# A decoder trunk in split float32: one more gate/up pair and branch pair by seven products, five raw weight buffers, 59 small slots

## The chip, the cores and the metric

The kernel runs on one core of a Trainium2 chip. The metric is the device time in microseconds (us) of one execution; of several executions the median is given. TensorE is called PE, VectorE DVE, ScalarE ACT, GpSimd POOL and SyncE SP, as in the profile.

## The reference, cut to what matters

Input is one sequence of 512 tokens of width 1024, in float32. There are two layers, and each has three sub-layers with an RMS norm before and after each:

```
x += 1/2 * post(SwiGLU_1(pre(x)))                 # FFN, D_FF = 2816
h  = pre(x);  P = h @ W_in                        # HGRN2 q/f/i/gate, attention q/k/v, branch gates gA, gB
A  = HGRN2 gated linear recurrence -> W_bA        # 4 heads, 128x128 state, chunks of 64
B  = sliding-window (128) attention -> W_bB       # 8 heads, 2 KV heads, ALiBi, sinks
x += post((sigmoid(gA)*A + sigmoid(gB)*B) @ W_out)
x += 1/2 * post(SwiGLU_2(pre(x)))                 # FFN

swiglu(h) = (silu(h @ w_gate) * (h @ w_up)) @ w_down
```

D_FF = 2816 gives 22 blocks of 128 (`FT`), and the width of 1024 gives 8 (`KT`).

## The kernel before, in words

**Numbers.** Every float32 product is made of three matmuls: both operands are split into a rounded high part and the rest, and high x high, low x high and high x low are summed (`mm3`; all go through L115). An operand is split by `split()`: ACT casts it to the high part (L400), DVE subtracts to get the low part (L401). Weights come in units of 128 x 1024, are loaded by SP into raw buffers (tag `w32`, `W32` = 4 of them, 512 KB each), and are split by the weight stream `Stream`: ACT casts (L324) into a `whi` tile, and the low part `wlo` is made by DVE (L331), or by ACT and an accumulating DMA of POOL (L328, L329). There are `WS` = 6 pairs of `whi` and `wlo`. Activations and all other small tensors live in slots of 128 x 512 float32 (`big()`, tag "s", 256 KB each, `SLOTS` = 61).

**An FFN.** `ffn()` first runs `quad()`: two gate/up pairs of output blocks at once, in plain form. A plain pair is two `project()` calls of 8 x 3 matmuls of 512 columns, 48 in all, followed by `gated()`. The first FFN goes on plainly to pair `FIRST` = 7, as its norm is not known yet; the three others to pair `PLAIN` = 4. All further pairs go by `sevenths()`, called from `fast()`: a 2x2 product of halves with seven products instead of eight, on sums of weights (items a, b, c, d of the stream; DVE makes the sums, L311 to L318) and on sums of the operand halves (`pre.sums()`, four times, once for each two blocks of the operand). A pair by sevenths is 7 x 4 x 3 = 84 matmuls of 256 columns. Its p1 is copied out of PSUM by ACT (L864); DVE adds the products (L874 to L882), ACT applies SiLU (L894), and DVE multiplies (L895).

**The down projection.** `down()` multiplies the 22 gated blocks by the down weights. `both(j, 0)` takes operand blocks 2j and 2j+1 against one weight unit, 24 matmuls of 512 columns. The first four of them are plain; then `quarters()` does eight blocks by seven products (items p1 to p7, split by `quarter()`, L281 for the high and L286 for the low halves; p1 needs two items); then come the remaining `both`. With the first of these units, 16 tiles of raw weights for the quarter products are loaded into small slots (the side loads, L252). The last sevenths splits the first `EARLY` = 4 operand blocks by `early()` (L892's argument), so that the first `both` has its operands:

```
            m = sevenths(pre, early)
```

**The mixer.** Its 8 output blocks have two branch gates each. For the attention branch the first `LATE` = 8 gates are plain (`branch`), and in pairs by `branches()` from there on; for the recurrent branch all go in pairs. Each pair by `branches()` uses `sevenths()`; the operand sums are made with the last four plain ones.

**The order.** The program is written in Python order, with coroutines (`order`) for what runs beside the matmuls. A scheduler then gives every instruction its place on its engine's queue, by priorities and by when slots of each tag come free; `pin()` raises the priority of a few. The engines run these queues in order, so a changed number of slots can change the order on ACT and DVE.

**The start.** Eight tiles of the input and the first weight units are loaded in turn, then the constants: `ident`, `half_ident` (two DMAs), `dist`, `mask`, `lb_in`, `hgh`, `sink`. The first FFN's squares (L430, L431), their sums by PE and the root (L443) give the norm, which enters at L904.

Of the kernel before, what the change touches and what calls it, by code (L numbers as in the profile page):

```python
# [15 lines left out]
P = 128  # L16
# [10 lines left out]
EPS = 1e-6  # L27
LEVELS = (1, 2, 4, 8, 16, 32, 64)
MASKS = [(m, n) for b in LEVELS[:-1:2] for m, n in ((b, b), (2 * b, 2 * b), (2 * b, b))] + [(64, 64)]
SLOTS = 61  # L30

WAIT = dict(
    first=0.0, spread=2300.0, squares=1700.0, lay=34500.0, laid=770.0, normed=7600.0, final=2600.0,
    head=2600.0, level=1720.0, chunks=1270.0, blocks=350.0, norm=2370.0, gate=8000.0,
    values=1200.0, scores=2000.0, exp=9000.0, shares=4500.0, turn=1900.0, turned=3000.0, rest=1200.0, lent=3500.0, apart=4000.0, block=2000.0, pair=4000.0, att0=1260.0, att1=12300.0,
)
W32, WS, AHEAD, TAIL, PLAIN, FIRST, EARLY, LATE = 4, 6, 3, 4, 4, 7, 4, 8
TURN = 0
LEAD = 8
ORDER = ("p1", "p6", "p2", "p7", "p5", "p4", "p3")  # L40
# [5 lines left out]
def trunk(ctx: ExitStack, tc: tile.TileContext, xin, wall, gains, lbT, hgain, sinks, c_dist, c_mask, c_ident, out):  # L46
    nc = tc.nc
# [11 lines left out]
    def nm(s):  # L59
        seq[0] += 1  # L60
        return f"{s}_{seq[0]}"

    def big(dt=F32, shape=None):
        return sb.tile(shape or [P, S], dt, tag="s", name=nm("s"), bufs=SLOTS)

# [9 lines left out]
    def const(shape, name, dt=F32):  # L75
        return cp.tile(shape, dt, tag=name, name=name)
# [738 lines left out]
    def quad(pre, halves):  # L815

        o = [acc() for _ in range(4)]
        blocks = {}
        ws.pinned = halves
        for half in (0, 1) if halves else (None,):  # L820
            c = WHOLE if half is None else HALF[half]
            for k in range(KT):
                order.until(lambda: pre.have[half or 0] > k)
                for j in range(4):
                    if (k, j) not in blocks:
                        blocks[k, j] = ws.next(uses=2 if halves else 1)
                    wmm(o[j][:, c], blocks[k, j], cut(pre.h[k], c), k == 0, k == KT - 1)
            ws.pinned = False
        return o

    def project(pre):
        o = acc()
        for k in range(KT):
            wmm(o, ws.next(), pre.h[k], k == 0, k == KT - 1)
        return o
# [49 lines left out]
    def fast(pre, a, start):  # L885
        def early():
            if j == FT - 1:
                for i in range(EARLY):
                    a[i] = split(a[i])

        for j in range(start, FT):
            m = sevenths(pre, early)  # L892
            z = big(F32, [P, 2, H2])
            nc.scalar.activation(out=m[:, 0:2, :], in_=m[:, 0:2, :], func=AF.Silu)  # L894
            nc.vector.scalar_tensor_tensor(z, m[:, 0:2, :], -1.0, m[:, 2:4, :], op0=ALU.mult, op1=ALU.mult)  # L895
            a.append(z.rearrange("p i t -> p (i t)"))

    def ffn(l, n, pre, nxt, halves=True):
        a = []

        def gated(og, ou):
            z, u = big(), big()
            if first:
                pin(nc.vector.tensor_tensor(z, og, pre.rb, op=ALU.mult))  # L904
                nc.scalar.activation(out=z, in_=z, func=AF.Silu)
                nc.vector.tensor_tensor(u, ou, pre.rb, op=ALU.mult)
                nc.vector.tensor_tensor(u, u, z, op=ALU.mult)
            else:
                nc.scalar.activation(out=z, in_=og, func=AF.Silu)
                pin(nc.vector.tensor_tensor(u, ou, z, op=ALU.mult))  # L910
            a.append(u)

        first = isinstance(pre, First)
        o = quad(pre, halves)
        if first:
            o.append(project(pre))
            order.until(lambda: pre.rb is not None)
        if not first:
            pre.sums()
            pre.sums()  # L920
        for j in range(2):
            gated(o[2 * j], o[2 * j + 1])
        if first:
            gated(o[4], project(pre))
            for j in range(3, FIRST):
                if j > 3:
                    order.until(lambda: pre.laid)
                    pre.sums()
                if j == 4:
                    pre.sums()  # L930
                gated(project(pre), project(pre))
            fast(pre, a, FIRST)
        else:
            for j in range(2, PLAIN):
                pre.sums()
                gated(project(pre), project(pre))
            fast(pre, a, PLAIN)
        return down(a, FT, l, n + 1, nxt, True)
# [349 lines left out]
    pre = First()  # L1288
# [4 lines left out]
            ws.load(k + 1)  # L1293
    ident = const([P, P], "ident")
    nc.sync.dma_start(ident, c_ident)
    half_ident = const([P, 64], "half_ident")
    nc.sync.dma_start(half_ident[:64], c_ident[:64, :64])
    nc.sync.dma_start(half_ident[64:], c_ident[64:, 64:])
    dist = const([P, 256], "dist")
    nc.sync.dma_start(dist, c_dist)  # L1300
    mask = const([P, len(MASKS) - 1, 32], "mask", I32)
# [5 lines left out]
    nc.sync.dma_start(hgh, hgain.partition_broadcast(P))  # L1307
    sink = const([P, DEPTH, NH], "sink")
    nc.sync.dma_start(sink, sinks.partition_broadcast(P))
    for k in range(KT):  # L1310
        pre.add(k)
        if k in (0, 2, 4):
            ws.split()
        if k > 2:
            pre.square(k - 3)
# [42 lines left out]
    for l in range(DEPTH):  # L1358
        pre = ffn(l, 0, pre, (l, 2), halves=l > 0)
        pre = mixer(l, pre, (l, 4))  # L1360
        pre = ffn(l, 4, pre, (l + 1, 0) if l + 1 < DEPTH else None)
# [81 lines left out]
```

## Time and profile before

| | us |
|---|---|
| median of 3 runs | 2112.13 (2110.0 to 2112.33) |
| profiled execution | 2114.98 |
| its span from first to last instruction | 2113.2 |
| PE busy | 2101.1 (99%) |
| DVE busy | 1551.0 (73%) |
| ACT busy | 1124.9 (53%) |
| mean granted clock of PE | 0.998 |

Times in rows count from the start of the span. In a timeline a row has the start, the length, engine, line, operation, output and input with sizes, the count, and in brackets the idle time of the engine before it with what ended that. Matmuls overlap, so a matmul's length is more than its distance to the next. A row of the chain of waits has the start, the length and the number of instructions in a row. The stages of layer 0, as the trace shows them: first FFN to about 345 us, mixer to about 700, second FFN to about 1045; layer 1 follows likewise.

### The profile page before, as it was taken

The numbers are of one execution on the slowest core, as the hardware profiler recorded it, in microseconds if no ns is written. First come the engines' busy times: TensorE is split into PE (matmuls) and PEld (weight loads), VectorE is DVE, ScalarE is ACT, GpSimd is POOL, SyncE is SP. The second block draws the span as 40 slices with busy tenths as digits, with TensorE's granted clock in tenths as the row PEclk, the third lists the DMA queues.
The fourth block names the chain that finished last, engine by engine and source line by source line (L and its number), as shares of the span: only waits on it lengthen the run. The fifth ranks groups of instructions, "written<-read, shape, count | busy, mean of one in ns | idle before, by whom it ended". The sixth has DMA issues, their size and how long they took to land.

```text
span 2113.2 us, 35244 instructions
## 1 busy us (share of the span) xinstructions
PE 2101.1 (99%) x13549; PEld 1875.3 (89%) x13549; DVE 1551.0 (73%) x2705; ACT 1124.9 (53%) x1900; POOL 154.6 (7%) x188
## 2 busy tenths in 40 slices
PE   9999999999999999999999999999999999999998
PEld 7899988887888999998899998888778989999987
DVE  5777886767676777779587778767686767777884
ACT  6555554446445555556355556454554545555562
POOL 0111000000000011110001110000000000111000
PEclk9999999999999999999999999999999999999999
DMA  7577754321237357774437775632122553677651
GB/s 234 150 181 181 188 146 137 106 70 61 70 100 209 120 125 175 180 194 125 160 109 175 181 185 150 189 116 95 51 71 70 135 185 110 154 182 181 183 165 45
DMA packets 148072, 298.36 MB, mean 141 GB/s; under 512 B 16992, under 2 KB 74816, under 8 KB 147904
## 3 DMA queue, kind: packets, MB, share of 16 engines
q1 hardware_dynamic: 122416, 228.16, 32.8%
q0 software_dynamic: 25344, 67.91, 18.5%
q8 instruction: 106, 1.74, 0.3%
q14 instruction: 62, 0.51, 0.1%
q10 hardware_dynamic: 144, 0.05, 0.0%
HBM read 213.43 MB, written 14.73 MB: 108 GB/s over the span
## 4 chain that ended last, share of the span: by engine, by line
PE 81%; DVE 9%; ACT 5%; issue 2%; DMA 2%; SPq 1%; ACTq 0%; DVEq 0%
PE acc L115 60%; PE aux L115 19%; ACT whi L324 2%; DMA w<-wall 2%; PE aux L125 1%; DVE s L401 1%; DVE wlo L331 1%; DVE wlo L286 1%; PE acc L125 1%; ACT s L400 1%; ACT m L894 1%; ACT wlo L328 1%; SPq L241 1%; DVE tt L268 0%; DVE w L267 0%
## 5 line engine op out<-in xcount | busy, mean ns | idle before, releaser
L115 PE MATMUL acc<-s,whi 128*128 128x256 f32 (+1 forms) x4968 | 1069.9, 312 | 1.7 <-ACT whi L324 0.9
L115 PEld LDWEIGHTS acc<-s,whi 128*128 128x128 f32 x4968 | 809.9, 191 | 54.5 <-issue 2.1
L115 PE MATMUL acc<-s,wlo 128*128 128x256 f32 (+1 forms) x2484 | 770.5, 310 | 0.1
L115 PEld LDWEIGHTS acc<-s,wlo 128*128 128x128 f32 x2484 | 474.5, 191 | 25.9 <-DVE wlo L331 0.4
L324 ACT CAST whi<-w 128x1024 fp32r<-128x1024 f32 (+1 forms) x341 | 317.4, 949 | 252.2 <-PE aux L115 103.4
L115 PE MATMUL acc<-whi,s 128*128 128x512 f32 x1264 | 413.6, 393 | 0.0
L324 ACT CAST whi<-tt 128x1024 fp32r<-128x1024 f32 x154 | 161.7, 1050 | 341.4 <-DVE tt L318 188.9
L331 DVE TENSOR_TENSOR wlo<-w,whi 128x1024 fp32r<-128x1024 f32 (+1 forms) x181 | 218.5, 1216 | 134.8 <-ACT whi L324 128.4
L115 PEld LDWEIGHTS acc<-whi,s 128*128 128x128 f32 x1264 | 237.0, 188 | 55.7 <-issue 3.2
L331 DVE TENSOR_TENSOR wlo<-tt,whi 128x1024 fp32r<-128x1024 f32 x154 | 188.2, 1222 | 102.5 <-ACT whi L324 102.5
L115 PE MATMUL acc<-wlo,s 128*128 128x512 f32 x632 | 246.8, 391 | 1.0 <-DVE wlo L286 1.0
L329 POOL DMA_DIRECT2D wlo<-w x160 | 138.2, 865 | 1266.3 <-ACT wlo L328 856.7
L115 PE MATMUL aux<-s,whi 128*128 128x256 f32 x1232 | 225.1, 283 | 0.0
L115 PE MATMUL aux<-whi,s 128*128 128x512 f32 x592 | 196.8, 390 | 0.0
L115 PEld LDWEIGHTS aux<-s,whi 128*128 128x128 f32 x1232 | 192.2, 192 | 0.0
L115 PE MATMUL aux<-s,wlo 128*128 128x256 f32 x616 | 174.4, 283 | 0.1
L115 PEld LDWEIGHTS acc<-wlo,s 128*128 128x128 f32 x632 | 118.7, 188 | 25.8 <-DVE wlo L286 2.4
L115 PEld LDWEIGHTS aux<-whi,s 128*128 128x128 f32 x592 | 111.1, 188 | 22.9
L328 ACT ACTIVATE wlo<-w 128x1024 fp32r<-128x1024 f32 (+1 forms) x160 | 129.9, 845 | 0.0
L400 ACT CAST s<-s 128x512 fp32r<-128x512 f32 (+1 forms) x164 | 88.6, 581 | 65.9 <-DVE s L459 60.6
L115 PEld LDWEIGHTS aux<-s,wlo 128*128 128x128 f32 x616 | 118.3, 192 | 0.3 <-DMA wlo<-w 0.3
L115 PE MATMUL aux<-wlo,s 128*128 128x512 f32 x296 | 115.2, 389 | 0.0
(185 smaller groups left out, 2136.6 us busy)
## 6 DMA issues: line engine op xcount, KB each, us to landing
w<-wall SPq DMA_DIRECT2D x267, 512.0 KB, 3.7
wlo<-w POOLq DMA_DIRECT2D x83, 512.0 KB, 5.5
w<-wall SPq DMA_DIRECT2D x288, 128.0 KB, 3.1
wlo<-w POOLq DMA_DIRECT2D x77, 256.0 KB, 3.3
x_d<-s SPq DMA_DIRECT2D x48, 256.0 KB, 2.1
s<-x_d SPq DMA_DIRECT2D x48, 256.0 KB, 5.5
w<-wall SPq DMA_DIRECT2D x34, 256.0 KB, 2.9
s<-wall SPq DMA_DIRECT2D x64, 128.0 KB, 3.5
```

Of the source, the lines that this page charges most:

```text
L115: nc.tensor.matmul(o, lhsT, rhs, start=start, stop=stop)
L125: nc.tensor.transpose(o, src, ident)
L241: nc.sync.dma_start(w.rearrange("p (m c) -> p m c", m=4) if c is None else w[:, c], a)
L286: nc.vector.tensor_tensor(it.lo[:, h[c]], w[c], it.hi[:, h[c]].bitcast(F32), op=ALU.subtract)
L324: i = nc.scalar.copy(it.hi[:, c], w[:, c])
L328: nc.scalar.mul(it.lo[:, c], w[:, c], -1.0)
L329: nc.gpsimd.dma_start(it.lo[:, c].bitcast(F32), w[:, c], accum_op=ALU.add)
L331: nc.vector.tensor_tensor(it.lo[:, c], w[:, c], it.hi[:, c].bitcast(F32), op=ALU.subtract)
L400: nc.scalar.copy(hi, src)
L401: nc.vector.tensor_tensor(lo, src, hi.bitcast(F32), op=ALU.subtract)
L894: nc.scalar.activation(out=m[:, 0:2, :], in_=m[:, 0:2, :], func=AF.Silu)
```

## The change

`PLAIN` goes from 4 to 3: the three FFNs other than the first have one plain pair less and one more by sevenths. The operand sums that went with the two plain pairs go with the one that is left. `LATE` goes from 8 to 6: each mixer has two plain attention gates less and one more pair by `branches()`. `W32` goes from 4 to 5, that is one more raw weight buffer of 512 KB, and `SLOTS` from 61 to 59, two slots of 256 KB less. With `W32` = 5 the loop at the start also issues one more weight unit among the input tiles. The two DMAs of `half_ident` are issued after all other constants.

```diff
-SLOTS = 61
+SLOTS = 59
...
-W32, WS, AHEAD, TAIL, PLAIN, FIRST, EARLY, LATE = 4, 6, 3, 4, 4, 7, 4, 8
+W32, WS, AHEAD, TAIL, PLAIN, FIRST, EARLY, LATE = 5, 6, 3, 4, 3, 7, 4, 6
...
             for j in range(2, PLAIN):
-                pre.sums()
+                while len(pre.x56) < min(4, 2 * j):
+                    pre.sums()
                 gated(project(pre), project(pre))
             fast(pre, a, PLAIN)
...
     ident = const([P, P], "ident")
     nc.sync.dma_start(ident, c_ident)
-    half_ident = const([P, 64], "half_ident")
-    nc.sync.dma_start(half_ident[:64], c_ident[:64, :64])
-    nc.sync.dma_start(half_ident[64:], c_ident[64:, 64:])
     dist = const([P, 256], "dist")
...
     nc.sync.dma_start(sink, sinks.partition_broadcast(P))
+    half_ident = const([P, 64], "half_ident")
+    nc.sync.dma_start(half_ident[:64], c_ident[:64, :64])
+    nc.sync.dma_start(half_ident[64:], c_ident[64:, 64:])
```

Lines of the kernel after are one higher than before from L932 on.

## The prediction

> **What bounds the kernel now.** I read the page's busy shares first, then TensorE's waits, then the chain of waits, and only then the timelines of the stages that the change touches.
>
> ```profile
> span 2113.2 us, 35244 instructions
> ...
> PE 2101.1 (99%) x13549; PEld 1875.3 (89%) x13549; DVE 1551.0 (73%) x2705; ACT 1124.9 (53%) x1900; POOL 154.6 (7%) x188
> ```
>
> ```profile
> engine line waited for: us in total, times, longest us
> PE acc L125 <- DVE s L730: 2.9, 1, 2.9
> PE aux L115 <- DVE s L431: 1.1, 1, 1.1
> ...
> PE acc L115 <- DVE wlo L286: 1.0, 4, 0.3
> ...
> PE acc L115 <- DVE s L904: 0.7, 1, 0.7
> ```
>
> PE is busy for 2101.1 of 2113.2 us, so time goes only by fewer or shorter matmuls, by removing the 12 us of stalls, or by making new stalls. The last is where the risk lies, as VectorE (DVE) and ScalarE (ACT) have idle time but feed PE just in time at a few places. The profiled execution took 2114.98 us, 2.85 above the median of 2112.13; I add the sum of differences to either, and state the result against the median.
>
> **Fewer matmul columns.** The order of PE's instructions in the two built kernels differs in five places only: 48 matmuls of 512 columns become 84 of 256 in the three FFNs that start from plain pairs, and in both mixers. The chain of waits prices both forms (start, length, matmuls):
>
> ```profile
> 772.07 7.20 PE acc L115 x60
> 779.27 2.88 PE aux L115 x24
> ...
> 987.92 5.44 PE aux L115 x24
> ```
>
> A pair by sevenths is 60 + 24 matmuls in 7.20 + 2.88 = 10.08 us (0.120 each). 24 matmuls of 512 columns take 5.44 us (0.2267 each), so a plain pair is 48 x 0.2267 = 10.88. Each swap saves 0.80 and five save **4.0 us**. This is certain as long as the feeding engines keep up. The Trainium skill ("TensorE: Matmul & The Clock Gate", "Back-to-back issue gap") gives N/2.4 + 2.5 ns for an isolated gap: 215.8 and 109.2 ns, from which I estimate 5.9 us for the five; the trace shows 226.7 and 120, and the rows decide.
>
> Can DVE feed the additional sevenths? In the FFNs and in the mixer:
>
> ```profile
> 900.00:910.00 10.00, 10.00 (x85) 10.00 (x85) 7.56 (x12) 5.83 (x8) 1.73 (x2) 1.00 0.77 182
> ```
>
> ```profile
> 743.40:761.99 18.59, 18.59 (x85) 15.39 (x84) 13.71 (x24) 8.44 (x12) 0.86 (x1) 1.00 0.12 34
> ```
>
> ```profile
> 743.44 1.28 DVE L563 TENSOR_TENSOR s<-s,s 128x512 f32<-128x512 f32 x2
> ...
> 747.76 0.69 DVE L311 TENSOR_TENSOR tt<-w,w 128x512 f32<-128x512 f32 x1
> ...
> 756.22 0.68 DVE L317 TENSOR_TENSOR tt<-tt,w 128x512 f32<-128x512 f32 x1
> ...
> 758.79 1.23 DVE L331 TENSOR_TENSOR wlo<-tt,whi 128x1024 fp32r<-128x1024 f32 x1 [1.17 <-ACT whi L324]
> ```
>
> ```profile
> 555.26 0.69 DVE L1091 TENSOR_REDUCE ss<-s 128x4 f32<-128x512 f32 x1 [3.72 <-ACT s L1089]
> ...
> 568.91 0.69 DVE L1091 TENSOR_REDUCE ss<-s 128x4 f32<-128x512 f32 x1 [5.04 <-ACT s L1089]
> ```
>
> The first two are windows (columns: length, then busy PE, PEld, DVE, ACT, POOL; granted clock; DMA share; GB/s), the others DVE's timeline. In steady sevenths DVE is busy 7.56 of 10 us, so it keeps up. The first sevenths of this FFN begins at 761.99 (the window's end), and one plain pair sooner, at 751.1, after the change. The operand sums of one pair take 743.44 to 747.76, 4.3 us; two in a row end at 752.1. The third weight item's own sums and split take 3.8 more (756.22 to 760.0), until 755.9; its product is the fifth of seven, and begins 4 x 10.08 / 7 = 5.76 us after the start, at 756.9. It fits with 1 us to spare. In the mixer the earlier sums fall into idle stretches of 3.72 and 5.04 us. I cost both at nothing; without that 1 us of cover, a stall of up to 1 us in each of three FFNs.
>
> **The start.** Startup ACT and PE rows (timeline: start, length, and in brackets the idle time before and its releaser):
>
> ```profile
> 22.73 1.05 ACT L324 CAST whi<-w 128x1024 fp32r<-128x1024 f32 x1 [4.35 <-DMA w<-wall]
> 24.01 1.06 ACT L324 CAST whi<-w 128x1024 fp32r<-128x1024 f32 x1 [0.23 <-DMA w<-wall]
> ```
>
> ```profile
> 32.99 1.05 PE L115 MATMUL aux<-ones,s 128*128 128x1 f32 x8 [1.09 <-DVE s L431]
> ```
>
> ```profile
> core 0: us, PE busy (x) PEld busy (x) DVE busy (x) ACT busy (x) POOL busy (x), PEclk, DMA share, GB/s
> ...
> 31.28:34.70 3.42, 2.33 (x15) 1.77 (x14) 1.62 (x3) 3.40 (x4) 1.41 (x2) 1.00 0.90 241
> 34.70:38.11 3.41, 3.41 (x10) 2.65 (x9) 0.87 (x2) 0.85 (x2) 0.46 (x1) 0.50 1.05 239
> 38.11:41.50 3.39, 2.68 (x10) 1.59 (x9) 1.29 (x2) 2.10 (x3) 0.00 (x0) 1.00 0.90 205
> ```
>
> The fifth weight unit arrives at 22.73, the sixth at 24.01; ACT's square and DVE's L431 queue behind them, and PE waits 1.09 us at 32.99. With five raw buffers the fifth unit is loaded with the first ones, so the sixth should land when the fifth does now: 24.01 - 22.73 = 1.3 us earlier. That covers the 1.09. A second price hangs on it: after the window with that stall (PE busy 2.33 of 3.42) the granted clock is 0.50 for one window of 3.41 us, which loses 3.41 / 2, about 1.6 us as the matmuls there are counted (10 instead of some 15). After a window busy 2.68 of 3.39 the clock stays 1.00. Gain: 1.1 + 1.6, less a longer wait for L904 (0.7 now), since PE arrives sooner: between 0 and 3.4, taken as **2.3 us**. The identity halves are loaded after the small constants and first used in the mixer, hundreds of us later: nothing.
>
> **The entry of the down projection, four times.** This is where the sum turns. With 59 small slots, and side loads that ask for slots one weight unit earlier, the built order on ACT and DVE changes at the end of the last sevenths, in all four FFNs alike. Before, ACT does: copy of p1 (L864), cast of a[0] (L400), unit 2 (L324), a[1], a[2], unit 3, a[3], and then the four half casts of the first two quarter items (L281). After: units 2 and 3, the four L281, and only then L864 and the four L400. On DVE the four L286 and L874 likewise stand ahead of the four L401. ACT and DVE run in order, so the down projection's operands now queue behind the L281. The second quarter item's cast waits for a `whi` buffer whose last reader is the last product of the last sevenths, and PE's next instruction needs a[0]. The rows of before, second FFN:
>
> ```profile
> 936.97 0.35 ACT L864 COPY s<-acc 128x256 f32<-128x256 f32 x1
> 937.22 0.62 ACT L400 CAST s<-s 128x512 fp32r<-128x512 f32 x1
> ...
> 941.79 1.05 ACT L324 CAST whi<-w 128x1024 fp32r<-128x1024 f32 x1 [1.96 <-DMA w<-wall]
> 942.75 0.62 ACT L400 CAST s<-s 128x512 fp32r<-128x512 f32 x1
> 943.27 0.62 ACT L281 CAST whi<-w 128x512 fp32r<-128x512 f32 x1
> 944.16 1.34 ACT L281 CAST whi<-w 128x512 fp32r<-128x512 f32 x2 [0.28 <-DMA w<-wall]
> 946.73 0.62 ACT L281 CAST whi<-w 128x512 fp32r<-128x512 f32 x1 [1.22 <-DMA w<-wall]
> ```
>
> ```profile
> 938.83 0.69 DVE L401 TENSOR_TENSOR s<-s,s 128x512 fp32r<-128x512 f32 x1
> ...
> 944.62 0.68 DVE L874 TENSOR_TENSOR m<-acc,s 128x512 f32<-128x512 f32 x1
> 945.22 1.89 DVE L286 TENSOR_TENSOR wlo<-w,whi 128x512 fp32r<-128x512 f32 x3
> ```
>
> ```profile
> 943.15 0.28 PE L115 MATMUL aux<-s,wlo 128*128 128x256 f32 x1
> 943.27 0.40 PE L115 MATMUL acc<-whi,s 128*128 128x512 f32 x1
> ...
> 943.74 0.62 PE L115 MATMUL acc<-whi,s 128*128 128x512 f32 x2
> ```
>
> Now a[0] is ready at 937.8 (high part) and 939.5 (low part), and PE passes into the down projection at 943.27 without a gap. After, in the same coordinates: the last product ends at 943.4, and the second item's two casts start at 943.45 and 944.2 to 944.5. The later one waits for its transfer, which a fifth buffer brings a unit earlier, to where the item before it has its wait now (944.16), a little later for a side load put ahead. It takes 0.62; L864 takes 0.25 of ACT and L400 0.62, so a[0]'s high part is there at 945.6 to 945.9. DVE does the last L286 at 944.8 to 945.1, L874 0.6 later, and L401 of a[0] another 0.6 later: low part at 946.7 to 947.0. PE's third matmul, at 943.74 now, needs it: a shift of 3.0 to 3.3, taken as **3.2 us**, some 2.4 of it in one piece. From below 2.2, if DVE does not bind; from above 5.5, if the transfer comes no earlier than now (946.73). Four times 3.2 is **12.8 us**. Given back: PE's four waits for L286 (1.0 in all, about 1.6 with the weight loads), since DVE has more lead then: **-1.6**.
>
> The stall also touches the clock. One idle stretch of 1.09 us cost a half-clock window above. So did the last wait:
>
> ```profile
> 2104.00:2107.00 3.00, 0.20 (x1) 0.00 (x0) 2.30 (x5) 1.02 (x3) 0.00 (x0) 0.93 0.57 175
> ```
>
> Here the clock falls within 3 us of idle. At 2.4 us in one piece and 0.7 more, each stall should be followed by a half-clock window (1.6 us); how the stall falls on the windows can spare one. I take three of four: **+4.8**, between 0 and 9.6 (two windows each). The Trainium skill ("TensorE: Matmul & The Clock Gate", "Why this matters for your kernels") says to have no idle gaps over about 3 us, by which gaps of 2.4 us would cost nothing more; the row at 31.28 speaks against it here.
>
> **Sum.** -4.0 - 2.3 + 12.8 - 1.6 + 4.8 = **+9.7 us**: 2124.7 for the profiled execution, 2121.8 against the median.
>
> **Rivals.**
> 1. The entry stalls come, but the clock stays (a window still counts as busy with 2.4 us idle): +9.7 - 4.8 = +4.9, 2117.0. For it: after 0.7 us idle the clock stayed. Against: the two rows above. By the skill's 3 us it would be this one. Chance 0.20.
> 2. Faster: the entry is covered. This needs a[0]'s cast ahead of 943.27, that is the second item's casts before about 942, by a buffer or a transfer that I have put too late. Then -4.0 - 2.3 with the L286 waits as now: -6.3, 2105.8. It decides from an entry stall below 1.6 us (four of them eat the 6.3). Against it: the buffer that the cast waits for is read until 943.27. Chance 0.14.
> 3. Slower still: the quarter item's transfer lands as late as now, 5.5 us each, with one clock window each: -4.0 - 2.3 + 22.0 - 1.6 + 6.4 = +20.5, 2132.6. Against: the built order on SyncE issues it a unit earlier. Chance 0.08.
> 4. The stalls are at their lower bound, 2.2, without the clock, and the start gains 3.4: -4.0 - 3.4 + 8.8 - 1.6 = -0.2, 2111.9. Chance 0.08.
>
> **How the numbers follow.** Forecast 0.50, rivals 0.20, 0.14, 0.08 and 0.08. A measurement of this kernel can tell about 0.2%, or 4.2 us, from no change. Faster than that: rival 2 (0.14) and a little of 4: 0.15. Same: most of rival 4 and half of rival 1: 0.17. Slower: the rest, 0.68. The range goes from 2108 (above rival 2, most of which it leaves out, below rival 4) to 2128 (3.5 us a stall, a clock window for all four and a second for one, the start gaining nothing: -4.0 + 14.0 - 1.6 + 8.0 = +16.4), leaving out rival 3. The likeliest case's own range is 2117 to 2128.
>
> **What would show it.** Right: PE's waits list four new ones of 2 to 3 us at the first matmul of the down projections, for ACT L400, and shorter ones for DVE L401; the L286 waits are gone; the clock is 0.5 in a window behind each entry; a sevenths pair still takes 10.08 us, and the wait for L431 at 33 us is gone. Wrong: ACT's L400 of a[0] ends before PE's last product of the last sevenths, or PE's busy time falls by other than 4 us apart from the clock.

## The result: 3.2% slower, and the profile after

The changed kernel took 2178.51 us in the median (2175.37 to 2182.08), against 2112.23 for before in the same executions. The ratio is 1.0316 (95% interval 1.0293 to 1.0339), slower by 66 us. The forecast was 2121.8, with a range of 2108 to 2128. One execution of the run e7 below (3737.6 us) and one of before beside e12 and e13 (2559.2) ran at a mean granted clock of 0.75 to 0.76, and all medians here leave them out. The profiled execution took 2175.55 us. Its page, and PE's waits (total, times, longest):

```profile
span 2173.8 us, 35753 instructions
...
PE 2113.3 (97%) x13729; PEld 1890.6 (87%) x13729; DVE 1574.3 (72%) x2745; ACT 1136.0 (52%) x1925; POOL 162.9 (7%) x198
```

```profile
PE acc L115 <- DMA wlo<-w: 27.3, 18, 4.8
PE acc L115 <- ACT s L400: 10.4, 4, 4.2
PE aux L115 <- ACT s L1049: 6.4, 4, 2.2
PE acc L125 <- DVE s L730: 2.8, 1, 2.8
PE aux L115 <- DMA wlo<-w: 2.8, 4, 1.1
PE acc L115 <- DVE s L401: 1.2, 3, 0.5
...
PE acc L115 <- DVE s L904: 0.7, 1, 0.7
```

Three groups of waits are new. The four waits for L400 and three for L401, at the entries of the down projections, were forecast. The other two are not in the prediction at all: 30 us for the low parts of weights, which come by POOL's accumulating DMA (L329), and 6.4 us in the mixers for L1049, a copy that attention's matmuls need. The waits for L431 and L286 are gone.

The forecast entry looks as described. ACT, then DVE, then PE in the second FFN:

```profile
963.13 1.14 ACT L281 CAST whi<-w 128x512 fp32r<-128x512 f32 x2 [1.82 <-PE aux L115]
964.52 1.14 ACT L281 CAST whi<-w 128x512 fp32r<-128x512 f32 x2 [0.25 <-PE aux L115]
965.57 0.36 ACT L864 COPY s<-acc 128x256 f32<-128x256 f32 x1
965.83 2.18 ACT L400 CAST s<-s 128x512 fp32r<-128x512 f32 x4
```

```profile
963.78 2.69 DVE L286 TENSOR_TENSOR wlo<-w,whi 128x512 fp32r<-128x512 f32 x4 [1.22 <-ACT whi L281]
966.38 0.69 DVE L874 TENSOR_TENSOR m<-acc,s 128x512 f32<-128x512 f32 x1
966.99 2.49 DVE L401 TENSOR_TENSOR s<-s,s 128x512 fp32r<-128x512 f32 x4
```

```profile
964.33 0.28 PE L115 MATMUL aux<-s,wlo 128*128 128x256 f32 x1
966.50 0.50 PE L115 MATMUL acc<-whi,s 128*128 128x512 f32 x1 [1.90 <-ACT s L400]
966.84 0.57 PE L115 MATMUL acc<-wlo,s 128*128 128x512 f32 x1
967.72 0.80 PE L115 MATMUL acc<-whi,s 128*128 128x512 f32 x1 [0.31 <-DVE s L401]
```

PE's first matmul of the down projection comes 2.2 us after the last of the sevenths, and its third at 967.72 instead of some 964.9 (964.33 and the 0.59 us that lie between the two in before): 2.8 us late, where 3.2 was forecast. The windows at the first FFN's entry show the clock's part (columns as in the prediction):

```profile
243.27:246.68 3.41, 1.64 (x6) 1.07 (x7) 3.07 (x6) 2.88 (x6) 0.00 (x0) 1.00 0.86 263
246.68:250.09 3.41, 3.41 (x10) 2.64 (x9) 2.62 (x6) 0.81 (x2) 0.00 (x0) 0.50 0.88 267
```

A window with PE busy for 1.64 of 3.41 us is followed by one at half clock. Ahead of its last matmuls, after has nine such windows, and before has one (at 34.70). Five follow the four entries, two the longer wait of each mixer (557.29 and 1639.31), and two the waits for low parts at 813.75 and 847.98.

PE's idle time grew from 12.1 to 60.5 us of the span, by 48.4, and its busy time by 12.2, in which the windows at half clock are counted. Where the 60.6 us between the two spans arise shows when each matmul of after is set beside the same one of before, as their order is the same but for the five swaps. The table gives how much later PE comes out of each part than it went in:

| part | forecast, us | after, us |
|---|---|---|
| start | -2.3 | -2.8 |
| entries of the four down projections, with the clock | +17.6 | +20.9 |
| rest of the down projections (the L286 waits) | -1.6 | -2.9 |
| mixers, with their two swaps | -1.6 | +9.1 |
| gate/up pairs of the last three FFNs, with their three swaps | -2.4 | +34.6 |
| last wait and what follows PE's last matmul | 0 | +1.7 |

### The profile page after: what moved, and what is told of

Its sections match the earlier page's. It is cut to its first block, busy times and chain, and to the rows that moved or that the text cites. A ratio compares the mean times of both kernels' runs of the same rounds, so it can differ in the third digit from the quotient of the medians.

```text
span 2173.8 us, 35753 instructions
## 1 busy us (share of the span) xinstructions
PE 2113.3 (97%) x13729; PEld 1890.6 (87%) x13729; DVE 1574.3 (72%) x2745; ACT 1136.0 (52%) x1925; POOL 162.9 (7%) x198
## 5 line engine op out<-in xcount | busy, mean ns | idle before, releaser
L115 PE MATMUL acc<-whi,s 128*128 128x512 f32 x1264 | 418.4, 398 | 11.6 <-ACT s L400 10.4
L324 ACT CAST whi<-tt 128x1024 fp32r<-128x1024 f32 x164 | 171.7, 1047 | 387.9 <-DVE tt L318 261.6
L331 DVE TENSOR_TENSOR wlo<-w,whi 128x1024 fp32r<-128x1024 f32 (+1 forms) x171 | 207.1, 1217 | 134.6 <-ACT whi L324 130.2
L331 DVE TENSOR_TENSOR wlo<-tt,whi 128x1024 fp32r<-128x1024 f32 x164 | 200.6, 1223 | 92.0 <-ACT whi L324 87.8
L329 POOL DMA_DIRECT2D wlo<-w x170 | 146.4, 863 | 1296.4 <-ACT wlo L328 857.1
L115 PE MATMUL aux<-s,whi 128*128 128x256 f32 x1312 | 239.8, 283 | 0.0
L115 PEld LDWEIGHTS aux<-s,whi 128*128 128x128 f32 x1312 | 204.6, 192 | 0.0
L115 PE MATMUL aux<-s,wlo 128*128 128x256 f32 x656 | 186.0, 284 | 2.8 <-DMA wlo<-w 2.8
L328 ACT ACTIVATE wlo<-w 128x1024 fp32r<-128x1024 f32 (+1 forms) x170 | 142.8, 847 | 0.0
L400 ACT CAST s<-s 128x512 fp32r<-128x512 f32 (+1 forms) x164 | 87.6, 579 | 85.0 <-DVE s L459 82.4
L115 PEld LDWEIGHTS aux<-s,wlo 128*128 128x128 f32 x656 | 125.9, 192 | 3.6 <-DMA wlo<-w 3.6
```

What stands on the lines that cost most here:

```text
L115: nc.tensor.matmul(o, lhsT, rhs, start=start, stop=stop)
L324: i = nc.scalar.copy(it.hi[:, c], w[:, c])
L328: nc.scalar.mul(it.lo[:, c], w[:, c], -1.0)
L329: nc.gpsimd.dma_start(it.lo[:, c].bitcast(F32), w[:, c], accum_op=ALU.add)
L331: nc.vector.tensor_tensor(it.lo[:, c], w[:, c], it.hi[:, c].bitcast(F32), op=ALU.subtract)
L400: nc.scalar.copy(hi, src)
```

## The experiments

All times are medians, and those of before, taken beside them, are 2111.4 to 2112.9. Differences to before, in us:

| kernel | time | difference | ratio, 95% interval |
|---|---|---|---|
| after | 2178.5 | +66 | 1.0293 to 1.0339 |
| e1: PLAIN = 3 alone | 2138.9 | +27.5 | 1.0114 to 1.0144 |
| e2: five raw buffers and 59 slots alone | 2124.3 | +13.0 | 1.0047 to 1.0077 |
| e3: LATE = 6 alone | 2121.3 | +9.9 | 1.0032 to 1.0062 |
| e4: after, SiLU behind the cast of a | 2181.4 | +70 | 1.0310 to 1.0344 |
| e5: e1, L874 behind L318 | 2119.2 | +6.3 | 1.0016 to 1.0039 |
| e6: after, L874 behind L318 | 2139.2 | +26.4 | 1.0115 to 1.0145 |
| e7: after, three orders | 2121.1 | +8.3 | 1.0024 to 1.0053 |
| e8: as e7, four buffers, 61 slots | 2126.5 | +13.6 | 1.0048 to 1.0078 |
| e9: five buffers, 59 slots, late identity halves and entry order, PLAIN = 4, LATE = 8 | 2108.4 | -4.5 | 0.9967 to 0.9985 |
| e10: e5 with three sums first | 2118.5 | +5.6 | 1.0015 to 1.0036 |
| e11: e9 with PLAIN = 3 as in e10 | 2113.1 | +0.2 | 0.9990 to 1.0008 |
| e12: after with LATE = 8 | 2154.4 | +41.9 | 1.0184 to 1.0221 |
| e13: after with four buffers, 59 slots | 2158.5 | +46.0 | 1.0200 to 1.0233 |

**e1, e2, e3: each constant by itself.** The edits are those of the change: `PLAIN = 3` with its loop; `W32 = 5` and `SLOTS = 59`; `LATE = 6`.

> Before with PLAIN = 3 alone (and the loop for the operand sums): four raw buffers, 61 slots, LATE = 8. Theory A, ACT's order: this constant alone makes 18 of the 45 SiLUs (L894) of the last three FFNs stand ahead of a later pair's cast of item a, so that its accumulating DMA starts late; the trace of after has 32 us of waits for wlo from that, in steps of three pairs. Expected here -2.4 for the columns, +32 for the waits and 3 to 7 for half-clock windows: about 2147 (2140 to 2155), waits for wlo from the DMA of over 25 us. Rival B, the fifth raw buffer: the accumulating DMAs are late because one more load of 512 KB stands before them; then with four buffers the waits are gone and this is 2112 - 2.4 = 2110.

> Before with five raw buffers and 59 slots alone. Theory A: the order at the entry of the down projection is this constant's, four entry stalls of 3.1 us with a half-clock window of 1.7 each, less 1.6 for the L286 waits and less 2.7 at the start: 2112 + 12.4 + 6.8 - 1.6 - 2.7 = 2127 (2122 to 2131); no waits for wlo in the steady pairs. Rival B: the waits for wlo are here, 2112 + 30 to 40 on top of the entries: over 2150.

> Before with LATE = 6 alone. Theory A: the operand sums come two gates sooner, their casts (L400) stand ahead of ACT's copy L1048, which attention's matmuls wait for: two stalls of 2.3 and 1.1 us in each mixer, and a half-clock window behind the longer, less 1.6 for the columns: 2112 + 6.8 + 3.4 - 1.6 = 2121 (2117 to 2123). Rival: the stalls in the mixers come from the raw buffers or slots, and LATE alone gives -1.6: 2110.6.

Measured: 2138.9, 2124.3 and 2121.3, or +27.5, +13.0 and +9.9. The last two are as theory A expected; e1 lies just below its theory's 2140 to 2155. Each has its own new waits and none of the others'. In e1:

```profile
PE acc L115 <- DMA wlo<-w: 17.9, 17, 1.4
...
PE aux L115 <- DMA wlo<-w: 2.4, 3, 1.2
```

So the waits for low parts come with PLAIN = 3 and four buffers (20 us here, less than the 25 expected of it), the entries with e2's five buffers and 59 slots, the mixers' waits with LATE = 6. Which of e2's two constants it is, e13 shows, which has the 59 slots with four buffers: its ACT does the L400 casts ahead of the L281 in the first and third FFN, as in before (L400 of a[3] at 241.16 and L281 from 241.85 on), and all but that of a[3] in the others, and PE has no wait for L400 at any entry. It is the fifth buffer; the prediction had put the entry's order down to the slots. In the mixer the operand sums' cast has moved ahead of the copy. ACT in before, where the copy (L1048 there) follows as soon as PE has its input ready:

```profile
551.01 0.59 ACT L1048 COPY s<-aux 128x512 f32<-128x512 f32 x1 [0.73 <-PE aux L115]
```

ACT, then PE, in after:

```profile
554.31 1.14 ACT L400 CAST s<-s 128x512 fp32r<-128x512 f32 x2 [3.25 <-DVE s L459]
555.35 0.58 ACT L1049 COPY s<-aux 128x512 f32<-128x512 f32 x1
```

```profile
555.98 2.19 PE L115 MATMUL aux<-s,s 128*128 128x128 f32 x14 [2.17 <-ACT s L1049]
```

ACT stood idle for 3.25 us waiting for DVE's sum, with a copy behind it that PE needed.

**e4: the SiLU.** In after every third pair of the last three FFNs has L894 ahead of the next cast of item a. The edit queues each SiLU behind that cast, with nothing else meant to change (cut to its main line; `finish()` holds the SiLU and L895):

```diff
         w = ws.whole()
         product(p1, w, 0, 1)
+        finish()    # SiLU and L895 of the pair before, issue_after(cast and negation of a)
```

> After, with the SiLU of each pair by sevenths (L894) queued on ACT behind the next traced cast pair of item a (it is traced after the first product of the following pair and ordered with issue_after). Everything else as after. Theory A: the 18 late casts are in time again, the waits for wlo go: 2178 - 32 - 3 to 7 = 2141 (2136 to 2146). Rival B: the order is innocent, the fifth buffer's loads slow the accumulating DMAs: no change, 2175 to 2180.

Measured: 2181.4, no gain. Theory A fell for the steady pairs: the waits were now spread over all pairs, 26 us in 42 waits, instead of every third. Rival B came near the time, but its reason fails as well, since e1 has these waits with four buffers.

**e5 and e6: the add inside the loop.** The split of weights is a chain in which ACT and DVE wait for each other. It closes upon itself from pair to pair, since both run their queues in order, and so forms a loop; a turn is the time from one instruction to the same one a pair later. The chain is: SiLU (L894), L895, L311, L312, cast of b, L331, L317, L318, cast of c, casts and negations of d and a, next SiLU. DVE in before:

```profile
865.60 0.69 DVE L895 SCALAR_TENSOR_TENSOR s<-m 128x512 f32<-128x512 f32 x1 [1.25 <-ACT m L894]
...
869.75 0.69 DVE L317 TENSOR_TENSOR tt<-tt,w 128x512 f32<-128x512 f32 x1
870.47 0.69 DVE L318 TENSOR_TENSOR tt<-tt,w 128x512 f32<-128x512 f32 x1
871.08 0.69 DVE L874 TENSOR_TENSOR m<-acc,s 128x512 f32<-128x512 f32 x1
...
875.81 0.69 DVE L895 SCALAR_TENSOR_TENSOR s<-m 128x512 f32<-128x512 f32 x1 [1.26 <-ACT m L894]
```

One turn is 875.81 - 865.60 = 10.21 us, and so are nearly all of before. That is 0.13 more than PE's 10.08: PE does not have to wait because the splits are ahead of it when the pairs begin, and each pair uses up some of that lead. In e1:

```profile
868.48 0.69 DVE L895 SCALAR_TENSOR_TENSOR s<-m 128x512 f32<-128x512 f32 x1 [1.64 <-ACT m L894]
...
872.64 0.68 DVE L317 TENSOR_TENSOR tt<-tt,w 128x512 f32<-128x512 f32 x1
873.24 0.68 DVE L874 TENSOR_TENSOR m<-acc,s 128x512 f32<-128x512 f32 x1
873.84 0.68 DVE L318 TENSOR_TENSOR tt<-tt,w 128x512 f32<-128x512 f32 x1
...
879.18 0.69 DVE L895 SCALAR_TENSOR_TENSOR s<-m 128x512 f32<-128x512 f32 x1 [1.64 <-ACT m L894]
```

The add L874, which only the pair's output needs, stands between L317 and L318 and lengthens the turn to 10.70. With the third pair's shorter turn the mean is 10.53 (three turns of 10.76, 10.70 and 10.13). PE has to wait 0.45 us a pair, in portions of three pairs. In e4's order another add stood there (L881, L884 in e4's kernel, 0.34 us to the next start), and its turns were 10.53 as well, which is why e4 gained nothing. The edit:

```diff
+        with tc.issue_after(ws.sum_c):    # the last L318 traced
             nc.vector.tensor_tensor(m[:, 0:4:2, :], pairs[0], ...)    # L874
```

> Before with PLAIN = 3, and the add L874 queued on DVE behind the weight sum of item c (L318) that was traced before it. Theory C: the split of a pair's weights is a loop of ACT and DVE (SiLU, L895, L311, L312, cast of b, L331, L317, L318, cast of c, casts and negations of d and a, SiLU), 10.21 us long in before and 10.5 on average with PLAIN = 3, since L874 (0.60) stands between L317 and L318; PE needs 10.08. With L874 behind L318 the loop is 10.2 again, the waits for wlo go, and the three swaps give their 2.4: 2111.4 - 2.4 = 2109 (2108 to 2111). Rival D: loads and accumulating DMAs collide because of where the pairs begin: 2135 to 2140 as without the edit.

> After with the same single edit. Theory C: the entries (13 us by the kernel with five buffers alone) and the mixers (10 us by the kernel with LATE = 6 alone) stay, the steady pairs lose nothing: 2111.4 + 13 + 10 - 2.4 = 2132 (2129 to 2136). Rival E: the 15 us by which after exceeds the sum of the single changes are the fifth buffer's loads, queued ahead of an accumulating DMA, whatever the order: 2147.

Measured: 2119.2 and 2139.2. e1's 27.5 fell to 6.3, after's 66 to 26.4. DVE in e5, where the add is L876:

```profile
865.66 0.69 DVE L897 SCALAR_TENSOR_TENSOR s<-m 128x512 f32<-128x512 f32 x1 [1.25 <-ACT m L896]
...
870.53 0.69 DVE L318 TENSOR_TENSOR tt<-tt,w 128x512 f32<-128x512 f32 x1
871.14 0.68 DVE L876 TENSOR_TENSOR m<-acc,s 128x512 f32<-128x512 f32 x1
...
875.86 0.69 DVE L897 SCALAR_TENSOR_TENSOR s<-m 128x512 f32<-128x512 f32 x1 [1.25 <-ACT m L896]
```

The turns are 10.20 again. This one place in DVE's order was 21 us by itself and 40 in the whole change. Both runs still missed what theory C expected: 2109 by 10 us, and 2132 (2129 to 2136) by 7, where rival E had 2147. In e5 the larger part is lost at the first pairs by sevenths. At that of the second FFN; ACT, POOL, PE:

```profile
752.10 0.61 ACT L325 CAST whi<-w 128x512 fp32r<-128x512 f32 x1
752.62 0.63 ACT L329 ACTIVATE wlo<-w 128x512 fp32r<-128x512 f32 x1
```

```profile
753.54 0.86 POOL L330 DMA_DIRECT2D wlo<-w  x1 [20.94 <-DVE wlo L332]
```

```profile
757.51 0.39 PE L115 MATMUL aux<-s,wlo 128*128 128x256 f32 x1 [1.02 <-DMA wlo<-w]
```

Item d's cast queues on ACT behind item c's, and its low part then takes an accumulating DMA, issued at 753.54 and waited for until 757.51. The prediction had checked item c and forgotten d. The waits for low parts still sum to 4.9 us in e5. Set beside before matmul by matmul, e5 loses 5.4 us at the three first pairs, their 2.4 us of columns counted, and 2.4 us at the last pair or the entry in the second and fourth FFN, for which no cause was sought.

**e7 and e8: all orders restored.** e7 adds the entry and the mixer to e6; e8 is the same with four buffers and 61 slots, where the entry needs no edit:

```diff
+                with tc.issue_after(self.behind):    # cast of a[3]
                     nc.scalar.copy(it.hi[:, h[c]], w[c])    # L281
...
-            if m >= LATE - 4:
+            if m >= LATE - 2:
+                pre.sums()
                 pre.sums()
```

> After with three edits to the order alone: L874 behind L318; the L281 casts of the quarter items behind the early cast of a[3]; the mixers' four operand sums with the last two plain gates, two each, instead of one each with the last four. If the three orders are the whole loss, the columns (-4.0) and the start (-2.7) remain, and the L286 waits may return (0 to +1.6): 2111.4 - 6.7 + 0.8 = 2105.5 (2103 to 2108). If something else of the change costs (contention of five buffers, 59 slots): above 2112.

> After with four raw buffers and 61 slots, L874 behind L318, and the mixers' sums as in e7. Columns -4.0, no gain at the start: 2111.4 - 4.0 = 2107.4 (2106 to 2109).

Measured: 2121.1 and 2126.5, or +8.3 and +13.6, where some -6 and -4 were expected. The waits for L400 at the entries and for the copy in the mixers are gone in e7, but low parts of weights are waited for again, 9.3 us in all: at the first pairs as in e5, and at the first pair of each mixer, where two sums on end now stand ahead of the splits (the place is seen in the trace, the cause argued). The order edits undo what they were made for, and more than the columns' 4 us is lost at the changed start of the pairs.

**e9, e10, e11: what can be kept.** e9 has the five buffers, the 59 slots, the late identity halves and the entry edit of e7, with PLAIN = 4 and LATE = 8. e10 is e5 with a third `pre.sums()` ahead of the first pairs, and e11 has both.

> After with PLAIN = 4 and LATE = 8 again and the L281 casts queued behind the early casts: what is left of the change is five raw buffers, 59 slots and the late identity halves, without the lost order at the entry. No new stalls at the entries; the start gains what it gained in after (2.7, of which 1.6 are one half-clock window that not every execution need have). 2112.8 - 2 = 2110.5 (2109 to 2112.5). If five buffers cost something besides the order at the entry: above 2114.

> The kernel with PLAIN = 3 and L874 behind L318, with three operand sums instead of two ahead of the first two pairs and one behind. It lost 6 us at the first pairs by sevenths. Theory: two sums in a row (8.6 us of DVE) put off c's weight sum, d's cast and so d's accumulating DMA, which lands 1.2 us too late (1.2 to 2.3 us a FFN); one sum sooner gives 4 us back there: 2119 - 6 - 0 = 2113 less what of 2.4 the columns give: 2110.5 (2109 to 2113). Rival: the added sum delays gated(), an accumulator is not free for the next pair, and PE waits there: 2119 or more.

> Both of the former at once: five raw buffers, 59 slots, late identity, L281 behind the early casts, PLAIN = 3 with L874 behind L318 and three sums first, LATE = 8. -2.4 for the columns and about -2 at the start: 2108.5 (2106.5 to 2112), the fastest of all if the parts add; over 2114 if the fifth buffer's loads still delay an accumulating DMA in the steady pairs.

e9 took 2108.4, a little better than its 2109 to 2112.5, and beats before (0.9976 of it) and after. All of PE's waits but four are gone:

```profile
PE acc L125 <- DVE s L732: 2.8, 1, 2.8
PE aux L115 <- DVE eps_t L138: 1.1, 1, 1.1
PE acc L115 <- DVE s L907: 0.7, 1, 0.7
PE acc L115 <- ACT whi L325: 0.3, 1, 0.3
```

The L286 waits are gone without any stall at the entry, so the stall is not what removes them; the prediction had put it down to the lead that the stall gives DVE. That it is the earlier transfers is argued. e10 took 2118.5, close to its rival's 2119: the waits for low parts fell from 4.9 to 2.5 us, but `gated()` came later and PE waited 2.5 us for its SiLU to free an accumulator. e11, which joins e9 and e10, took 2113.1, where 2106.5 to 2112 was expected, and ends where before is. PE's waits in e10:

```profile
PE acc L115 <- ACT s L911: 2.5, 3, 1.4
PE aux L115 <- DMA wlo<-w: 1.5, 2, 1.2
```

**e12 and e13: the rest of the 66.** The three constants alone sum to 50.4.

> After with LATE = 8. If the missing 15 us belong to five raw buffers together with PLAIN = 3 (loads of the fifth buffer stand ahead of late accumulating DMAs, which then land 8 instead of 5 us later): 2112.5 + 27.5 + 13 + 15 = 2168 (2164 to 2172). If they belong to LATE = 6 with one of the others: 2112.5 + 27.5 + 13 = 2153.

> After with four raw buffers and still 59 slots. If the fifth buffer is the partner: the entries' 13 and the 15 go, 2112.5 + 27.5 + 10 = 2150 (2146 to 2153). If the 59 slots are: only the entries go, 2165.

e12 is +41.9, with e1 and e2 at 40.5, so those two add little to each other; this is the second answer expected of it. e13 is +46.0, 8.6 more than e1 and e3, and lies between its two answers. So some 9 of the missing 16 us come with LATE = 6 and PLAIN = 3 without the fifth buffer (e13 keeps the 59 slots, which no run has alone) and 1 with the buffer and PLAIN = 3. The other 6 need the buffer together with LATE = 6; no run has those two without PLAIN = 3. Set beside before, the place is the pairs of the second FFN, which lose 14.8 us in after and 16.4 in e13, but 7.0 in e1 and 6.5 in e12. The rows that go with it, in after, POOL, SP and PE:

```profile
805.00 0.88 POOL L329 DMA_DIRECT2D wlo<-w  x1 [2.23 <-ACT s L864]
```

```profile
805.27 0.33 SPq L244 DMA_DIRECT2D w<-wall  x1
```

```profile
813.75 0.58 PE L115 MATMUL acc<-s,wlo 128*128 128x256 f32 x1 [4.85 <-DMA wlo<-w]
```

A raw load of 512 KB was issued while POOL was still busy with its accumulating DMA (0.88 us), and PE got that low part 8.75 us after its issue; the median from issue to landing is 5.5. In e13, with four buffers, the same occurs at 799.03 and 799.28, and PE waits 4.5 us until 807.44. The fifteen traces bear the reading out. Of 1292 accumulating DMAs of 512 KB, the 668 with no load of 256 KB or more issued within 2 us land 5.5 us after their issue in the median. Twenty have exactly one such load from 2 us before to 2.5 us after their issue, and it comes 0 to 0.8 us after it: the five with the load within 0.35 us took 6.9 to 8.7 us, the fifteen with it 0.6 to 0.8 us behind took 6.0 to 7.0. Such a collision needs a phase between the loop and the loads, and LATE = 6 shifts what precedes the FFN. Why it shifts the phase in this direction was not shown, and no run delayed the loads alone, so that the load is the cause of the late landing stays argued.

## Why the prediction was wrong, point by point

**Columns, -4.0: right.** After has 240 matmuls of 512 columns less and 420 of 256 more. Their median distance to the next start is 227 and 120 ns in both profiles, which gives 54.5 us less and 50.4 more: -4.1.

**The start, -2.3: right in size, in part by luck.** The cast of the sixth unit starts at 22.77 in after and 24.01 in before, 1.24 us earlier where 1.3 was forecast, and the wait for L431 is gone in after, e7, e9 and e11. But e6 and e12, with the same edits at the start, still wait 0.7 and 0.5 us for it. And the 1.6 us of the window at half clock seem not to be in every execution of before: 31 of its 48 beside e1 to e13 have a mean granted clock of 0.998 and a median of 2113.3, the other 17 have 0.999 and 2111.7. The profiled one lay 2.85 us above the median, so this part of the sum should not have been taken from the median as well. In e1, which starts as before with the same wait (1.10 us, to 33.24), the clock stays full:

```profile
29.90:33.31 3.41, 2.31 (x11) 1.57 (x10) 3.25 (x5) 3.41 (x5) 0.65 (x1) 1.00 0.86 276
33.31:36.72 3.41, 3.41 (x19) 2.98 (x20) 0.84 (x2) 2.47 (x3) 1.21 (x2) 1.00 0.96 233
```

The clock changes only in steps of 3.413 us, which lie elsewhere in each execution (last section). In before one step, from 31.28 to 34.70, holds both the wait and the eight matmuls of one column behind it. In e1 a boundary at 33.31 parts them (614 steps before its change of clock at 2129.09).

**The entries, +12.8 and +4.8: right in mechanism, and nearly in size.** Waits for L400 and L401 are 11.6 us in after, five half-clock windows follow the four entries (three were taken), and the entries cost 20.9 us there and 17.7 in e2, for the 17.6 of the sum. The cause was misnamed: it is the fifth buffer, not the 59 slots (e13). That the clock did fall behind waits of 1.9 to 4.2 us decides against rival 1, and against the Trainium skill's "No PE-idle gaps >~3µs" ("TensorE: Matmul & The Clock Gate", "Why this matters for your kernels"). It does not fall behind each: the entry of e2 at 946.73 waited 1.9 us without it. Of the steady pairs' waits, those of 1.1 to 1.4 us in e1 were not followed by such windows; in after those of 4.85 and 2.46 were, and those of 1.71 and 3.42 were not. The -1.6 for the L286 waits was too small: the rest of the down projections is 2.9 us shorter in after, and in e9 too.

**"DVE is busy 7.56 of 10 us, so it keeps up": this step failed, by 21 to 40 us, and is the main one.** The term was put at nothing, and the gate/up pairs lost 34.6 us instead of gaining 2.4. A busy share says nothing of a loop over two in-order engines. DVE had 2.4 us idle a pair, yet the loop of ACT and DVE took 10.21 us against PE's 10.08, so there was no room at all; an add moved by one place made it 10.5. Putting that one add back gave 21 us by itself (e1 to e5) and 40 in the whole change (after to e6). The place stood in the built order, which the prediction used for the entries and not for the steady pairs.

**"It fits with 1 us to spare": failed, by some 5 us in all.** The first pair's item d, with the DMA of its low part, was left out (e5, e10).

**The mixer at nothing: failed, by some 11 us.** The mixers lost 9.1 us instead of gaining 1.6; LATE = 6 alone costs 9.9 (e3). DVE's idle stretches were there, but the sums' casts go through ACT's queue, ahead of a copy that PE waits for.

**Range and rivals.** None of the rivals had any of these three. All were variations of the one place that had been found, so the range was too narrow above. Ahead of the prediction `pin()` is said to raise a priority; in the kernel it is `tc.keep_in_program_order`, which keeps an instruction in the order in which it was traced.

## What to carry to other kernels

Where two in-order engines feed each other, add up the loop from one instruction to the same one of the next round, waits included, and compare it with the period of the engine that must not wait: a busy share of 75%, as DVE's here, can hide a loop with no slack. A change of loop counts or buffers can reorder every queue that a scheduler fills, so compare the built orders in the steady state too, at each place, and price what now stands ahead of what. Where such an order matters, state it (here by one `issue_after`), and keep the parts that gain by themselves: e9 has the fifth buffer with the entry's order and is 0.24% faster than before.

## What the runs showed of the hardware

**Accumulating DMAs.** One of 512 KB that lands 5.5 us after its issue in the median landed 8.7 us (after) and 8.4 us (e13) after it when a load of 512 KB was issued 0.25 to 0.27 us behind it. With the load 0.6 to 0.8 us behind, fifteen took 6.0 to 7.0 us.

**The clock.** Within an execution, the granted clock changes only at points that lie whole multiples of 3.413 us apart: in before at 34.70, 38.11 and, 606 steps later, 2106.59; in after at 246.68 and, 91 steps later, 557.29. Where these points lie differs from one execution to the next. The first 100 and the last 75 us left out, the fifteen traces have 32 steps at full clock in which PE was busy for less than 1.57 us, and half clock followed each. It followed 3 of 10 with 1.58 to 1.78 us and none of some 8500 with 1.89 us or more. So here the busy share of a step, and not the length of one wait, tells whether the clock falls: the 3.42 us wait in after that ends at 1958.39 fell on two steps, busy for 1.63 and 1.78 us, and cost no clock. The two exceptions are in the first 100 us, in before and e3 (2.33 and 2.41 us busy, half clock behind both). Of their busy time 1.05 us are the eight matmuls of one column, which the profile counts as busy; that the clock does not count them so is an inference.
